# A fused two-block transformer kernel: where the modulation passes stand, a merge in two passes, earlier recurrence gates, and other seams

## The chip, the core and the metric

The kernel runs on one NeuronCore of a Trainium2 chip. A core has five engines with instruction streams of their own: TensorE (PE, matrix products), VectorE (DVE), ScalarE (ACT), GpSimd (POOL) and SyncE (SP, which only issues transfers here). They meet through semaphores. The metric is the device time of one execution in microseconds (us), lower is better.

## What is computed

One sequence of 512 positions with 1024 channels passes through two blocks. Everything is float32.

```python
h  = modulate(rms(x, norm1_g), sh1, sc1); p = h @ w_in      # mod = silu(c) @ w_mod + b_mod
q, k, v = mla_qkv(p, ...)                                   # 8 heads, keys of the context beside them
x = x + g1 * ((sig(p_ga) * (attend(q, k, v) @ w_o) + sig(p_gb) * (fft2(p_f) @ w_fourier)) @ w_out)
h2 = modulate(rms(x, norm2_g), sh2, sc2)
x = x + g2 * expert_choice(h2, w_router, w_e_gate, w_e_up, w_e_down)   # 16 experts, 64 tokens each
z = rms(x, norm1_g_2) @ w_in_2                              # second block
u = causal_dwconv(z_x, 4) + b;  r, i = sig(u @ wa + ba), sig(u @ wx + bx)
y = [rg_lru(u, r, i) * gelu(z_gate), z_b * causal_dwconv(z_c * z_sx, 3)]
x = x + y @ w_out_2
x = x + (gelu(dwconv(gate)) * dwconv(up)) @ w_down_2;  out = rms(x, final_g_2)
```

## The kernel before

Each float32 factor of a large product is split into a high part, which ACT casts, and the rest, which DVE subtracts (`split`, and `Stream.ahead` for weights that come tile by tile: `w.h` is the `wih`, `w2h` of the trace, `w.l` is `wil`, `w2l`). `mm3` (L138) then makes three matmuls of each product, low times high, high times high, high times low (L141 to L143). A tile of 128 output channels by 512 positions is 24 matmuls of 512 columns, and needs both parts of its weights. The order on every engine is the order in which the code is written, and each engine executes its own stream strictly in that order.

`mix_in` (from 110 to 256 us) makes the tiles of `w_in`: `fcol(0..3)`, then `gate(8..15)`, each through `mtile` (L523), with the steps of q, k and v between them (`nat`, `s2`, `s3`, `s4`) and, between the gates, the two steps of the Fourier part (`ustep`, `ystep`). Beside that DVE makes 32 modulation passes: `mod_rest` (L455) fetches the vector c over ACT's queue as `sc`, ACT takes its sigmoid (`sce`), and each call of `parts` multiplies one row block `wm` of `w_mod` with `sc` and sums it into `mo` (L481). Three buffers of `wm` are in flight; SP fetches the next when a pass has freed one. `finish` adds the bias, turns `mo` on PE (L496) and stores rows that `merge` reads later.

`attention` follows, with `fourier(m)` (the Fourier output product) in its first part; `merge` (372 to 438 us) multiplies by `w_o` and `w_out`; then router, top-16 selection, gather, and 16 experts in pairs, whose weights stream in as tiles over SP's queue: 41 of them are issued at fixed points before the indices are known (`EW`, `ew_issue`), the others after. `scatter_last` closes the experts and prepares the second block's input.

`mix2` starts with eight tiles of the recurrence (`lru_in`, L1514): product, bias and convolution of four taps (ACT, then three DVE steps), split of the result, and three tiles later `gates` (six matmuls, two sigmoids, one product). There are two PSUM banks for `gates` and six for tiles. `short` makes the short convolutions, `lru1`, `lru2` the scan, `gated(0..7)` the last eight tiles. `ffn` makes 48 tiles and then the down product with eight accumulating banks.

All SBUF tiles are placed by hand: `PLAN` holds one address for each allocation, and a tile that takes memory of an older one waits for the older one's last reader.

## Time and profile before

| | us |
|---|---|
| median of 3 runs (1351.0 to 1352.37) | 1351.12 |
| the profiled execution | 1354.08 |
| its span | 1352.3 |
| PE busy | 1276.3 (94% of the span) |
| DVE busy | 720.6 (53%) |
| ACT busy | 509.0 (38%) |

The profiled execution is 3.0 us longer than the median, and 1.8 us of it lie outside the span. PE is the engine that is nearly always busy, so the 76 us in which it is not, and the stretches in which its clock is granted at half (PEclk 0.50, which is 1.2 GHz instead of 2.4), are what can be had back without removing work. A row of the waits names the instruction that waited, the instruction that released it, and the time. An engine other than PE matters where PE waits for it.

### The profile page before, as it was taken

The numbers are of one execution on the slowest core, as the hardware profiler recorded it, in microseconds if no ns is written. First come the engines' busy times: TensorE is split into PE (matmuls) and PEld (weight loads), VectorE is DVE, ScalarE is ACT, GpSimd is POOL, SyncE is SP. The second block draws the span as 40 slices with busy tenths as digits, with TensorE's granted clock in tenths as the row PEclk, the third lists the DMA queues.
The fourth block names the chain that finished last, engine by engine and source line by source line (L and its number), as shares of the span: only waits on it lengthen the run. The fifth ranks groups of instructions, "written<-read, shape, count | busy, mean of one in ns | idle before, by whom it ended". The sixth has DMA issues, their size and how long they took to land.

```text
span 1352.3 us, 16175 instructions
## 1 busy us (share of the span) xinstructions
PE 1276.3 (94%) x6418; PEld 962.8 (71%) x6418; DVE 720.6 (53%) x1099; ACT 509.0 (38%) x873; POOL 95.8 (7%) x141
## 2 busy tenths in 40 slices
PE   6999989999999399999888999999999999999997
PEld 4798867777687233433348888788988888878886
DVE  5646687678783612322257745843555555555323
ACT  5634442367633311111034466432333333344302
POOL 1223300000330000000010000000000000000002
PEclk9999989899999699999989999999999999999999
DMA  9510368220464999999950213330423202403201
GB/s 388 199 41 32 125 221 331 91 94 8 155 249 168 335 350 415 421 421 421 421 240 1 81 44 130 120 140 0 187 94 156 94 8 118 155 16 125 104 22 63
DMA packets 42844, 229.32 MB, mean 170 GB/s; under 512 B 5120, under 2 KB 5904, under 8 KB 23184
## 3 DMA queue, kind: packets, MB, share of 16 engines
q1 hardware_dynamic: 38736, 217.99, 41.4%
q10 hardware_dynamic: 2816, 6.08, 1.2%
q0 software_dynamic: 1216, 4.20, 0.9%
q8 instruction: 51, 0.84, 0.3%
q14 instruction: 25, 0.20, 0.0%
HBM read 224.05 MB, written 4.21 MB: 169 GB/s over the span
## 4 chain that ended last, share of the span: by engine, by line
PE 68%; DMA 8%; DVE 6%; ACT 3%; issue 1%; SPq 0%; POOLq 0%; POOL 0%; ACTq 0%; DVEq 0%
PE o L141 6%; PE o L143 6%; PE o L142 6%; PE mm L143 4%; PE mm L141 4%; PE mm L142 4%; DMA w_eu<-in_w_eu_dram 4%; PE d L1298 3%; PE u L142 3%; PE u L143 3%; PE u L141 3%; PE g L143 3%; PE g L142 3%; PE g L141 3%; DMA w_ed<-in_w_ed_dram 3%; PE g L1265 3%
## 5 line engine op out<-in xcount | busy, mean ns | idle before, releaser
L143 PE MATMUL mm<-hTh,w2l 128*128 128x512 f32 (+1 forms) x256 | 93.8, 367 | 2.5 <-DVE w2l L243 2.5
L141 PE MATMUL mm<-hTl,w2h 128*128 128x512 f32 (+1 forms) x256 | 94.2, 368 | 0.9 <-DVE hTl L150 0.8
L142 PE MATMUL mm<-hTh,w2h 128*128 128x512 f32 (+1 forms) x256 | 93.6, 365 | 0.0
L143 PE MATMUL g<-hTh,wul 128*128 128x512 f32 (+1 forms) x208 | 77.6, 373 | 0.5 <-DVE wul L243 0.5
L141 PE MATMUL g<-hTl,wuh 128*128 128x512 f32 (+1 forms) x208 | 77.6, 373 | 0.0
L143 PE MATMUL u<-hTh,wul 128*128 128x512 f32 (+1 forms) x208 | 77.6, 373 | 0.0
L141 PE MATMUL u<-hTl,wuh 128*128 128x512 f32 (+1 forms) x208 | 77.6, 373 | 0.0
L142 PE MATMUL g<-hTh,wuh 128*128 128x512 f32 (+1 forms) x208 | 77.5, 373 | 0.0
L142 PE MATMUL u<-hTh,wuh 128*128 128x512 f32 (+1 forms) x208 | 77.5, 373 | 0.0
L141 PE MATMUL o<-wdl,gsh 128*128 128x512 f32 x192 | 74.8, 389 | 1.1 <-DVE cv L1724 1.1
L142 PE MATMUL o<-wdh,gsh 128*128 128x512 f32 x192 | 74.7, 389 | 0.0
L143 PE MATMUL o<-wdh,gsl 128*128 128x512 f32 x192 | 74.7, 389 | 0.0
L1724 DVE SCALAR_TENSOR_TENSOR cv<-u,pvt,cv 128x510 f32<-128x510 f32 (+1 forms) x48 | 36.0, 749 | 65.5 <-ACT cv L1721 64.6
L1265 PE MATMUL u<-w_eu,xeT 128*64 128x512 f32 x256 | 58.9, 594 | 5.7 <-DMA w_eu<-in_w_eu_dram 5.7
L1265 PE MATMUL g<-w_eg,xeT 128*64 128x512 f32 x256 | 59.7, 603 | 2.7 <-DMA w_eg<-in_w_eg_dram 2.6
L1298 PE MATMUL d<-w_ed,ehT 128*64 128x512 f32 x256 | 59.4, 610 | 2.7 <-ACT ehT L1284 2.4
L1724 DVE SCALAR_TENSOR_TENSOR cv<-g,pvt,cv 128x510 f32<-128x510 f32 (+1 forms) x48 | 35.9, 749 | 45.4 <-ACT cv L1721 44.5
L243 DVE TENSOR_TENSOR wul<-wur,wuh 128x1024 fp32r<-128x1024 f32 x48 | 58.3, 1217 | 2.2 <-ACT wuh L242 1.8
L1275 DVE TENSOR_TENSOR h<-h,u 128x512 f32<-128x512 f32 x8 | 5.5, 688 | 96.7 <-PE u L1265 96.7
L143 PEld LDWEIGHTS mm<-hTh,w2l 128*128 128x128 f32 x256 | 49.1, 192 | 11.1 <-DVE w2l L243 3.5
L143 PE MATMUL mm<-hTh,wil 128*128 128x512 f32 x128 | 52.1, 407 | 5.0 <-DVE wil L243 5.0
L141 PE MATMUL mm<-hTl,wih 128*128 128x512 f32 x128 | 52.3, 409 | 4.0 <-ACT wih L242 4.0
(437 smaller groups left out, 3047.2 us busy)
## 6 DMA issues: line engine op xcount, KB each, us to landing
w_eg<-in_w_eg_dram SPq DMA_DIRECT2D x24, 1024.0 KB, 15.6
w_eu<-in_w_eu_dram SPq DMA_DIRECT2D x24, 1024.0 KB, 17.0
w_ed<-in_w_ed_dram SPq DMA_DIRECT2D x24, 1024.0 KB, 19.8
wur<-in_w_up_dram SPq DMA_DIRECT2D x24, 1024.0 KB, 6.0
wm<-in_w_modT_dram SPq DMA_DIRECT2D x32, 512.0 KB, 5.2
w2r<-in_w_in_dram SPq DMA_DIRECT2D x14, 1024.0 KB, 5.9
wdr<-in_w_down_dram SPq DMA_DIRECT2D x12, 1024.0 KB, 4.8
wir<-in_w_inT_dram SPq DMA_DIRECT2D x10, 1024.0 KB, 7.2
```

Of the source, the lines that this page charges most:

```text
L141: mm(ps, ah, bl, start=first, stop=False)
L142: mm(ps, ah, bh, start=False, stop=False)
L143: mm(ps, al, bh, start=False, stop=last)
L243: (lo or K.nc.vector).tensor_sub(w.l, src, w.h.bitcast(F32))
L1265: nc.tensor.matmul(p[64 * e:64 * e + 64, :], xT[:, k, 64 * e:64 * e + 64], w[e + k // m * 2][:, 512 * (k % m):512 * (k % m) + 512], start= ...
L1275: nc.vector.tensor_tensor(h, h, ps["w_eu"], op=OP.mult)
L1298: nc.tensor.matmul(p[64 * e:64 * e + 64, 512 * n:512 * n + 512], hT[:, k, 64 * e:64 * e + 64], w[k // m * 2 + e][:, 1024 * (k % m) + 512 * ...
L1724: nc.vector.scalar_tensor_tensor(v[:, s:T], ps[:, 0:T - s], f[:, k:k + 1], v[:, s:T], op0=OP.mult, op1=OP.add)
```

## The change

No arithmetic is taken out. What moves:

- `mod_rest` (the fetch of `sc`, its sigmoid and product) is called after `nat(3)` instead of at the third step of the `fcol` loop; the first three `wm` loads stay at that step (`mod_first`). The 32 passes stand between a tile's weight split and its eviction: none, none, one, three in `fcol(0..3)`, one in `gate(8)`, three in each of `gate(9..15)`, and the last six in `fourier(0..5)`. The bias follows `fourier(5)`, the turn of `mo` (`mod_finish`) the fifth attention item.
- The raw weights of `w_in` are loaded a tile earlier; `cpos` is loaded at step 3 and split after `gate(8)`; the tile pool of this part has four banks instead of three.
- `merge` makes the first half of `w_out`'s columns in two passes over the four banks; the splits and the routing steps are spread anew, and `EW` changes its portions (41 in both).
- `idle` issues five and later three matmuls that nothing reads, after the router rows and after the index matmuls.
- `scatter_last` splits the second tile of `w_in_2` ahead of `rows(2)` and `rows(3)`. In `lru_in`, `gates(j - 3)` stands right behind the tile's product, ahead of its convolution. One more tile of `w_in_2` is split ahead of the square roots. In the last stage the eight banks are used in another order.
- `PLAN` is new throughout.

On ACT, after `nat(3)` (`kT` copies the turned keys out of the bank `tr`, `v` is the value copy), before:

```order
L578 ACTIVATE sq_1085,s_124_1086<-a_1035 128x32
L697 ACTIVATE kT_1099<-tr_1103,pvt 96x2x128
L697 ACTIVATE kT_1100<-tr_1103,pvt 96x2x128
L697 ACTIVATE kT_1101<-tr_1103,pvt 96x2x128
L697 ACTIVATE kT_1102<-tr_1103,pvt 96x2x128
L610 COPY v_643<-a_1121 128x512
L614 ACTIVATE sq_1136<-a_1121 128x512
```

and now:

```order
L586 ACTIVATE sq_1087,s_125_1088<-a_1037 128x32
L462 DMA sc_1105<-in_crow_dram 128x1024
L463 ACTIVATE sce_1106<-sc_1105 128x1024
L705 ACTIVATE kT_1110<-tr_1114,pvt 96x2x128
L705 ACTIVATE kT_1111<-tr_1114,pvt 96x2x128
L705 ACTIVATE kT_1112<-tr_1114,pvt 96x2x128
L705 ACTIVATE kT_1113<-tr_1114,pvt 96x2x128
L618 COPY v_643<-a_1132 128x512
L622 ACTIVATE sq_1147<-a_1132 128x512
```

The fetch and the sigmoid that waits for it stand ahead of the four copies out of `tr`; before, they stood 42 rows later.

On DVE, at `gate(8)` (`wm` is a modulation pass, `cpl` the split of `cpos`, `wil` the split of a `w_in` tile, `ul` the Fourier part), before:

```order
L481 SCALAR_TENSOR_TENSOR wm_1569,mo_1559<-wm_1569,sc_1560 128x1024
L481 SCALAR_TENSOR_TENSOR wm_1657,mo_1559<-wm_1657,sc_1560 128x1024
L481 SCALAR_TENSOR_TENSOR wm_1660,mo_1559<-wm_1660,sc_1560 128x1024
L174 TENSOR_TENSOR cpl_1740<-cpr_1737,cph_1739 128x1024
L174 TENSOR_TENSOR cpl_1746<-cpr_1743,cph_1745 128x1024
L243 TENSOR_TENSOR wil_1757<-wir_1662,wih_1756 128x1024
L481 SCALAR_TENSOR_TENSOR wm_1729,mo_1559<-wm_1729,sc_1560 128x1024
L481 SCALAR_TENSOR_TENSOR wm_1732,mo_1559<-wm_1732,sc_1560 128x1024
L150 TENSOR_TENSOR ul_1795<-u_1793,uh_1794 128x1024
```

and now:

```order
L243 TENSOR_TENSOR wil_1745<-wir_1581,wih_1744 128x1024
L481 SCALAR_TENSOR_TENSOR wm_1670,mo_1104<-wm_1670,sc_1105 128x1024
L174 TENSOR_TENSOR cpl_1781<-cpr_1661,cph_1780 128x1024
L174 TENSOR_TENSOR cpl_1785<-cpr_1663,cph_1784 128x1024
L150 TENSOR_TENSOR ul_1790<-u_1788,uh_1789 128x1024
L243 TENSOR_TENSOR wil_1806<-wir_1748,wih_1805 128x1024
L481 SCALAR_TENSOR_TENSOR wm_1673,mo_1104<-wm_1673,sc_1105 128x1024
L481 SCALAR_TENSOR_TENSOR wm_1676,mo_1104<-wm_1676,sc_1105 128x1024
L481 SCALAR_TENSOR_TENSOR wm_1751,mo_1104<-wm_1751,sc_1105 128x1024
L153 SCALAR_TENSOR_TENSOR y4l_1337<-mm_1844,y4h_1336 128x2x256
```

One pass, not three, and the two `cpl` splits now precede the `ul` and the split of the next tile; the next three passes stand behind that split.

On ACT, in the recurrence's input loop (`gt` are the gate sigmoids, `xi` the tile's eviction, `xihlh` its cast, `w2h` the cast for the tile after next), before:

```order
L1517 ACTIVATE xi_5671<-mm_5397,pvt 128x512
L1520 CAST xihlh_5676<-xi_5671 128x512
L1523 CAST lwh_5392<-lwr_5390 128x256
L1535 ACT_TABLE_LOAD
L1535 ACTIVATE gt_5686<-gt_5682,pvt 128x512
L1535 ACTIVATE gt_5692<-gt_5688,pvt 128x512
L242 CAST w2h_5698<-w2r_5532 128x1024
L1517 ACTIVATE xi_5726<-mm_5695,pvt 128x512
```

and now:

```order
L1574 ACT_TABLE_LOAD
L1574 ACTIVATE gt_5684<-gt_5680,pvt 128x512
L1574 ACTIVATE gt_5690<-gt_5686,pvt 128x512
L1556 ACTIVATE xi_5693<-mm_5406,pvt 128x512
L1559 CAST xihlh_5698<-xi_5693 128x512
L1562 CAST lwh_5401<-lwr_5399 128x256
L242 CAST w2h_5707<-w2r_5541 128x1024
L1574 ACTIVATE gt_5739<-gt_5735,pvt 128x512
L1574 ACTIVATE gt_5745<-gt_5741,pvt 128x512
```

The table load and the two sigmoids moved ahead of the eviction of the fourth tile (`xi_5671`, now `xi_5693`), and the cast `w2h` moved behind that tile's casts.

The diff, cut to its core (of `PLAN` one line of each side):

```diff
 ARENA = 204 * 1024
-EW = (13, 4, 4, 6, 12, 0, 2)
+EW = (16, 4, 5, 3, 11, 0, 2)
...
-        def finish(P, tag):
+        def bias():
...
             nc.vector.scalar_tensor_tensor(mo[:, 2], mo[:, 2], 1.0, self.pv("n2g"), op0=OP.add, op1=OP.mult)
+        def finish(P, tag):
...
-        for _ in range(3):
-            load()
+        def first():
+            for _ in range(3):
+                load()
         self.sh2c, self.a2c = mo[:, 1], mo[:, 2]
-        return parts, finish
+        self.mod_parts, self.mod_bias, self.mod_finish, self.mod_first = parts, bias, finish, first
...
-        def mtile(i, P):
+        def mtile(i, P, parts=0):
             w = wst.get(i)
+            if i % 2 == 0:
+                wst.load(i // 2 + 1)
+            if parts:
+                self.mod_parts(parts)
...
-        def gate(i, P):
-            self.sigmoid(i, mtile(i + 4 * (i // 8), P))
+        def gate(i, P, parts=0):
+            self.sigmoid(i, mtile(i + 4 * (i // 8), P, parts))
...
-            ps = mtile(8 + g, P)
+            ps = mtile(8 + g, P, (0, 0, 1, 3)[g])
...
             A.free(w)
+        self.mod_rest()
...
                 f(t)
-            if i > 2:
-                parts(i - 1)
+            if i == 3:
+                cpr = [self.load(I["cpos"][b], [128, 2, 512], "cp") for b in range(2)]
...
                 A.free(wq, wkv)
-                parts, finish = self.mod_rest()
+                self.mod_first()
...
         A.free(tabs, rg, gq)
-        cp = [self.split(I["cpos"][i], [128, 2, 512], "cp") for i in range(2)]
...
         st = ExitStack()
-        P = Psum(self.tc, st, "pF", {"mm": (1, 3), "u": (2, 2), "m": (1, 1)})
+        P = Psum(self.tc, st, "pF", {"mm": (1, 4), "u": (2, 2)})
...
         for i in range(8):
-            gate(8 + i, P)
-            parts(2)
+            gate(8 + i, P, 3 if i else 1)
+            if i == 0:
+                cp = [self.split(None, [128, 2, 512], "cp", raw=r) for r in cpr]
+            if i == 6:
+                wfs = self.Stream(self, [I["w_fourier"][i] for i in range(2)], 4, "wfo", look=2)
+                wfs.load(0)
+                wfs.load(1)
+            if i == 7:
+                wfs.ahead(1)
             (ystep if i % 2 else ustep)(i // 2)
-            parts(2)
...
                 A.free(self.hTb, *cp)
-                wfs = self.Stream(self, [I["w_fourier"][i] for i in range(2)], 4, "wfo", look=2)
-                wfs.ahead(1)
-        finish(P, "m")
...
                 w = self.wfs.get(m)
+                if m < 6:
+                    self.mod_parts(1)
...
                 fourier(m)
+                if m == 5:
+                    self.mod_bias()
...
                     soft(items[i + 2])
+                if i == 4:
+                    self.mod_finish(P, "pt")
...
                     mgsplit(m - 1)
-                if m >= 4:
+                if m in (5, 7):
...
-            def out(t, n, lo, hi, steps):
-                ps = P("o")[:, 0:hi - lo]
+            def out(t, n, lo, hi, steps, ks=range(NK)):
+                if ks[0] == 0:
+                    acc[t] = P("o")
+                ps = acc[t][:, 0:hi - lo]
                 c, d = slice(128 * (t % 2), 128 * (t % 2) + 128), slice(lo, hi)
-                for k in range(NK):
+                for k in ks:
...
                     self.mm3(ps, m.h[:, c], m.l[:, c], w.h[:, k % 2, d], w.l[:, k % 2, d], k == 0, k == NK - 1)
+                if ks[-1] < NK - 1:
+                    return
...
+            acc = {}
+            for t in range(NT):
+                out(t, 0, 0, 512, {2: [(wsplit, t // 2)]}, range(NK // 2))
+            A.free(*wout[0][0:2])
...
                     steps = {k: [] for k in range(NK)}
-                    if (n, t) != (0, 0):
-                        u, b = (t - 1, n) if t else (NT - 1, 0)
-                        steps[4].append((route, u, 4 * b, 4))
-                        steps[7].append((route1, u, 4 * b))
+                    for k, f, u, b in {(0, 2): [(5, route, 0, 0)], (0, 3): [(4, route1, 0, 0), (5, route, 1, 0)],
+                                       (1, 0): [(0, route1, 1, 0), (1, route, 2, 0), (4, route1, 2, 0), (5, route, 3, 0)],
+                                       (1, 1): [(0, route1, 3, 0), (4, route, 0, 4), (7, route1, 0, 4)],
+                                       (1, 2): [(4, route, 1, 4), (7, route1, 1, 4)],
+                                       (1, 3): [(4, route, 2, 4), (7, route1, 2, 4)]}.get((n, t), []):
+                        steps[k].append((f, u, b, 4) if f is route else (f, u, b))
                     if n == 0:
-                        steps[1].append((wsplit, 1))
-                        out(t, 0, 0, 512, steps)
-                        if t == 1:
+                        if t % 2 == 0:
+                            steps[5].append((wsplit, 1))
+                        out(t, 0, 0, 512, steps, range(NK // 2, NK))
+                        if t == 0:
...
                         if t == NT - 1:
-                            for w in wout[0]:
-                                A.free(w)
+                            A.free(*wout[0][2:4])
...
             self.probe("x1", x)
+            warm = next(iter(self.ew.values()))
+            def idle(n):
+                ps = P("mm")
+                for _ in range(n):
+                    nc.tensor.matmul(ps, self.ident, warm[:, 0:512], start=True, stop=True)
+            idle(5)
...
                 nc.vector.tensor_copy(la[q], pa[q, 0:2 * NE].rearrange("p (b j i) -> p i b j", b=2, i=2)[:, i])
+            idle(3)
...
                 self.n_turn(P, "tr", 1, self.hTg)
+                self.ws2.ahead(1)
...
                 rows(3)
-                self.ws2.ahead(1)
...
                 ps = mtile(j)
+                if j > 2:
+                    gates(j - 3)
...
                 lru_in(j)
-                if j > 2:
-                    gates(j - 3)
...
                 lru1(2 * j + 1)
-            ws.ahead(22)
+            ws.ahead(23)
+            ws.look = 2
...
             P = Psum(self.tc, st, "pJ", {"o": (1, 8)})
-            acc = [[P("o") for n in range(2)] for t in range(NT)]
+            acc = [P("o") for i in range(2 * NT)]
+            acc = acc[:2] + acc[3:] + acc[2:3]
+            acc = [acc[2 * t:2 * t + 2] for t in range(NT)]
...
 PLAN = [
-    1, 299, 308, 25, 175, 242, 341, 316, 358, 33, 9, 220, 267, 283, 59, 139, 143, 0, 58, 333, 99, 266, 49, 376, 144, 1,
...
+    0, 352, 137, 129, 216, 8, 161, 145, 360, 260, 286, 328, 53, 200, 70, 258, 284, 179, 285, 9, 95, 8, 178, 216, 376,
...
```

## Rows read from the trace of the kernel before

**Rows 1.** PE's waits, whole run: engine, line, releaser: us in total, times, longest.
```profile
PE mm L143 <- DVE wil L243: 5.0, 5, 3.2
PE mm L141 <- ACT wih L242: 4.0, 3, 2.4
PE gt L141 <- ACT gt L1535: 2.9, 1, 2.9
PE m L496 <- DVE mo L491: 2.7, 1, 2.7
PE mm L143 <- DVE w2l L243: 2.5, 2, 1.7
```
**Rows 2.** Timeline of PE: start, us, instruction [idle before, releaser]; three waits of mix_in.
```profile
172.11 0.61 PE L141 MATMUL mm<-hTl,wih 128*128 128x512 f32 x1 [2.41 <-ACT wih L242]
...
194.35 0.50 PE L143 MATMUL mm<-hTh,wil 128*128 128x512 f32 x1 [3.23 <-DVE wil L243]
194.68 0.39 PE L141 MATMUL mm<-hTl,wih 128*128 128x512 f32 x1
194.91 0.39 PE L142 MATMUL mm<-hTh,wih 128*128 128x512 f32 x1
...
235.66 0.50 PE L141 MATMUL mm<-hTl,wih 128*128 128x512 f32 x1 [1.19 <-ACT wih L242]
```
**Rows 3.** Timeline of ACT around the modulation vector.
```profile
169.76 1.06 ACT L463 ACTIVATE sce<-sc 128x1024 f32<-128x1024 f32 x1 [5.74 <-DMA sc<-in_crow_dram]
```
**Rows 4.** Stretches: bounds, us, busy PE, PEld, DVE, ACT, POOL, PEclk, DMA share, GB/s.
```profile
172.40:179.20 6.80, 6.29 (x15) 4.41 (x15) 5.96 (x19) 3.01 (x6) 0.00 (x0) 0.50 0.80 298
257.70:261.10 3.40, 3.40 (x10) 2.62 (x9) 1.10 (x3) 3.40 (x7) 1.37 (x2) 0.50 0.02 2
372.00:438.00 66.00, 65.73 (x345) 51.74 (x343) 38.68 (x55) 22.58 (x46) 12.70 (x15) 1.00 0.57 205
448.84:472.73 23.89, 5.16 (x23) 3.03 (x25) 15.67 (x72) 6.62 (x15) 1.32 (x2) 0.50 0.97 347
474.00:484.00 10.00, 10.00 (x50) 3.23 (x46) 0.00 (x0) 0.61 (x2) 1.78 (x2) 1.00 0.81 284
742.40:745.80 3.40, 3.31 (x8) 2.63 (x9) 2.51 (x3) 2.23 (x4) 0.00 (x0) 0.50 0.00 0
```
**Rows 5.** Timelines of ACT, then PE, at the point to which mod_rest goes.
```profile
118.33 1.54 ACT L697 ACTIVATE kT<-tr,pvt 96x256 f32<-96x256 f32 x4
...
122.47 0.71 PE L594 MATMUL tr<-ident,craw 128*128 128x128 f32 x5
```
**Rows 6.** DMA issued in 1205 to 1222: queue, count, KB each, us to landing.
```profile
fg<-in_fg_dram ACTq DMA_DIRECT2D x1, 512.0 KB, 3.5
```
**Rows 7.** Groups of DVE in 168 to 256.43: count, busy us, mean ns, idle before.
```profile
L481 DVE SCALAR_TENSOR_TENSOR wm<-wm,sc 128x1024 f32<-128x1024 f32 x32 | 37.8, 1215 | 0.0
```
**Rows 8.** Timelines of ACT, DVE and PE in the input loop of the recurrence.
```profile
740.46 1.28 ACT L1535 ACT_TABLE_LOAD   x1
741.75 1.26 ACT L1535 ACTIVATE gt<-gt,pvt 128x512 f32<-128x512 f32 x2
...
743.98 1.23 DVE L243 TENSOR_TENSOR w2l<-w2r,w2h 128x1024 fp32r<-128x1024 f32 x1 [0.24 <-ACT w2h L242]
...
745.22 0.63 PE L141 MATMUL mm<-hTl,w2h 128*128 128x512 f32 x1
```
**Rows 9.** Timeline of DVE at the start of the second block.
```profile
713.33 1.22 DVE L243 TENSOR_TENSOR w2l<-w2r,w2h 128x1024 fp32r<-128x1024 f32 x1
```
**Rows 10.** Timelines of PE and DVE at the recurrence's output.
```profile
853.97 0.50 PE L143 MATMUL mm<-hTh,w2l 128*128 128x512 f32 x1 [1.75 <-DVE w2l L243]
...
857.67 1.20 DVE L243 TENSOR_TENSOR w2l<-w2r,w2h 128x1024 fp32r<-128x1024 f32 x1
```
**Rows 11.** Timeline of PE at the last stage's start.
```profile
1215.79 0.47 PE L141 MATMUL o<-wdl,gsh 128*128 128x512 f32 x1 [1.08 <-DVE cv L1724]
```
**Rows 12.** Timeline of PE at the experts' first work.
```profile
468.74 1.97 PE L1244 MATMUL tr<-ident,xe 128*128 128x128 f32 x8 [6.08 <-DMA xe<-h2d,idx]
```

86 rows, old and new, of the table PLAN are left out of this document.

## The prediction

> **What bounds the kernel now.** I first read the grouped waits of PE [rows 1], since the kernel spends 1276.3 of its 1352.3 us with PE busy, and then followed each long wait into the timelines of the engine that released it. Five groups belong to the places that the change touches: the weight splits of `mix_in` (5.0 and 4.0 us), the turn of `mo` (2.7), the recurrence gates (2.9) and the splits of the second block's input tiles (2.5, of which 1.75 is one wait [rows 10]). A sixth is the 1.08 us at the start of the last stage [rows 11]. Then I looked at the granted clock: after the longer waits there are stretches at 0.50 [rows 4], in which a busy PE does half its work. The 6.80 us behind the 2.41-us wait at 172.11 cost 3.1 us, since PE was busy for 6.29 of them; the 3.40 us behind the turn of `mo`, and a like stretch at 237.21 behind a wait for a split, cost 1.7 each. Everything below is counted on PE's path; DVE and ACT count where PE waits for them.
>
> **Modulation passes in `mix_in`.** The work is the same 32 passes of 1.2 us [rows 7], so only their places matter. The wait at 172.11 [rows 2] goes back to ACT, which had stood 5.74 us for the fetch of `sc`, until 169.76 [rows 3], with PE's next weights to be cast behind that. With the fetch made earlier, this wait goes, and its clock loss. The 3.23 us at 194.35 [rows 2] come from three passes and two `cpl` splits that stood ahead of a needed `wil`; the two splits, 2.4 us, now follow that `wil`, and what the three passes leave of the wait is in the cost below. The third wait, 1.2 us at 235.66, with its half clock, came from four passes a gate, and there are three now. The turn of `mo` leaves PE's path, since attention hides it: 2.74 us and its half clock. Removed: 2.4 + 3.2 + 1.2 + 2.7 = 9.5 us of waits, and 3.1 + 1.7 + 1.7 = 6.5 us of clock, 16.0 in all. The other 2.1 us of the three groups [rows 1] are waits of 0.2 to 0.5 us between steps that depend on each other; I leave them.
>
> What it costs: ACT now issues the fetch right after the last square of `nat(3)`, at about 118.4, and waits. Queued behind it are the four copies that empty the bank `tr` (1.54 us from 118.33 [rows 5]), and PE's transposes of `s2(2)`, at 122.47 in the same bank, wait for these. A fetch of the same size over the same queue, on quiet DMA, landed in 3.5 us [rows 6]; beside other loads ACT stood 5.7 for it [rows 3]. With the first, the sigmoid (1.06 us) ends at 123.1, the copies at 124.6, and PE waits 2.2 us; with the second, 4.4. I take 2.2, as few loads run there. Waits of 2.4 and 2.7 us were followed by half clock, so I add 1.7. Second, DVE still has one pass, two `cpl` splits and `ul` ahead of the `wil` of `gate(9)`, some 4.8 us, and three passes ahead of the one before; the nearest row is the 3.23-us wait with five such steps in front, the other end is nothing; I take 1.5, somewhat under half. Later gates carry five steps of 1.2 us each (three passes, one `wil`, one `ul`), against two 24-matmul groups and more of PE's in the time of two gates: DVE ends ahead. The six passes in attention lie beside softmax work with three banks to run ahead, so nothing. Sum: 16.0 - 2.2 - 1.7 - 1.5 = **10.6 us less** (bounds 6 and 14).
>
> **Merge and router.** The stretch 372 to 438 has PE busy for 65.73 of 66.00 us [rows 4]. The same products in another order can't gain there, and the moved splits have the DVE and ACT time (38.68 and 22.58 of 66) to hide in: nothing, bounds 0 and +1. If that cover failed, it would cost one split, 1.2 us, at each pass. The `idle` matmuls lie inside the waits for the selection (the whole stretch 448.84 to 472.73 has PE busy for 5.16 us only) and for the gather (6.08 us [rows 12]); eight 128-column transposes take 1.97 us at half clock [rows 12], so 512 columns take some 1.0, and five and three of them fit. They could give back the clock for the first 4.0 us of experts, 2.0 us. But after the last of the three PE would still stand idle for about 3 us before the gather lands, and waits of 2.4 us and more had half clock behind them. I take nothing, bounds 0 and -2.0.
>
> Here the Trainium skill ("TensorE: Matmul & The Clock Gate", Part 1) speaks for the idle matmuls: the throttled state is the default, and activity releases it. By that rule the sum would be 2.0 us lower.
>
> **Experts.** The stream has holes after the indices: in 474 to 484 the DMA share is 0.81 [rows 4], which is 1.9 us of stream lost, and it thins before and after. With the new addresses the first loads after the indices wait for earlier experts' readers. PE later waits for that stream, so what is filled comes back. I take most of the 1.9, **1.5 us less**; bounds 0 and -3.8, twice the 1.9.
>
> **`scatter_last`.** Of the 2.5 us for `w2l` [rows 1], 2.5 - 1.75 = 0.76 are here. The second tile's split moves ahead of the rows, which shift by its 1.2 us, and with them their squares, on ACT and POOL, the scaled rows, and the split at 713.33 [rows 9] that stands behind them. That third split, done at 714.55, was wanted at once. PE arrives 0.76 us sooner and waits 0.7 there: **0.1 less**, bounds -0.8 and +0.5.
>
> **Gates ahead of the convolution.** The 2.9-us wait [rows 1] was for the first two sigmoids, and those now come early enough. But look at what is late next. PE's following tile needs `w2h`, cast on ACT, and `w2l` from DVE, done at 743.98 + 1.23 = 745.21, and PE began that tile at 745.22 [rows 8]. On ACT the same steps stand ahead of `w2h` in both orders: table load 1.28, two sigmoids 1.26, eviction, convolution, casts; they are only permuted. So `w2l` is again done at about 745.2. PE makes its gates 2.9 us sooner, starts the tile's first two products when `w2h` is there, and then stands. It is ahead by two matmuls, 0.5 us, and the half clock [rows 4], which before fell on the gates while `w2l` was late anyway, now falls on the tile, 1.1 us for the 2.2 us left of it. I take **0**, bounds -1.7 and +1.2. Had the wait simply gone, it would be 2.9 + 1.7 = 4.6.
>
> In this chain the sigmoid starts 0.01 us behind the end of the table load [rows 8]. The Trainium skill ("ScalarE: Activation LUTs", "What ACT_TABLE_LOAD costs") counts a drain of 1.38 us to a table switch beside the load's 1.28. The row shows no such drain ahead of the sigmoid. By the page an estimate of the sum would be 1.4 later, 1339.6; I give that 0.03, inside the forecast.
>
> **One more tile ahead of the square roots.** It removes the 1.75 us [rows 10], and pushes the square roots and everything behind them on ACT by one cast, about the 1.06 us of ACT's step of that size [rows 3]. The next tile's `w2l` still ends at 857.67 + 1.20 = 858.9, behind the same chain, and PE, 1.75 us earlier, wants it after 24 matmuls of 0.23 each (the starts at 194.68 and 194.91 [rows 2]): 853.97 - 1.75 + 5.6 = 857.8. It waits 1.1: **0.7 less**, bounds -1.8 and 0.
>
> **Last stage.** The 1.08 us [rows 11] were the third bank's, which waits for the last tile's convolution. The code puts the third allocated bank last, but banks are handed out as they come into use: in the program as built the third accumulation still writes the bank of that last tile and carries the same wait. **0**, bounds 0 and -1.1.
>
> **The sum**: -10.6 - 1.5 - 0.1 - 0 - 0.7 - 0 = -12.9 us. On the profiled execution: 1354.08 - 12.9 = 1341.2. That execution stands 3.0 above the median, so on the median 1351.1 - 12.9 = **1338.2**.
>
> **Rivals.** (a) Every removed wait is a full gain: 4.6 at the gates, 1.75 for the split ahead, 0.76 in `scatter_last`, 1.1 in the last stage, 8.2 together where I count 0.8, and the early fetch costs no clock (1.7): 1338.2 - 7.4 - 1.7 = 1329.1. For it: each edit has its wait in the rows. Against: the chains above. Chance 0.17. (b) The cover in the gates runs out: three passes ahead of an eviction hold a bank or `ul`, 0.8 us in each of eight gates, 6.4 in all: 1344.6. For it: DVE was the releaser of 5.0 us there already. Against: four passes a gate before, three now, and one bank more. Chance 0.20. (c) The idle matmuls bring back the clock: 2.0 less, 1336.2; chance 0.15, inside the forecast's range. (d) Slower: the new addresses. SP issues in order, and a `wm` load that waits for its buffer holds the `w_in` tile queued behind it. Four such tiles lie in the gates. If each lands late as `wil` was at 194.35, 3.2 us and 1.7 of clock, that is 4 x 4.9 = 19.7: 1357.9. It decides from 12.9 / 4 = 3.2 us for each tile. For it: all addresses are new. Against: the tiles are asked for one earlier, and DMA carries a pass less a gate. Chance 0.06. (e) The gains of `mix_in` are met by a wait that I don't see in attention, and little is left: 1349 to 1353, chance 0.06.
>
> **How the numbers follow.** My forecast, with (c) in it, holds 1333 to 1342 with 0.51. The range takes in (a) and (b): 1329 to 1345, leaving out (d), (e) and the edges of the others. A measurement of this kernel tells 0.2%, 2.7 us, from no change. Faster: 0.17 + 0.51 + 0.20 = 0.88; within: 0.06; slower: 0.06.
>
> **What would show it.** Right: no PE wait over 1 us between 160 and 256 but one at `gate(9)`; a new wait of about 2 us at `s2(2)`, released by the `kT` copies; the 2.9-us wait gone from `gt` and a like one on the next tile's `w2h` and `w2l`; the 1.08 us still at the last stage. Wrong: waits of every gate on `wil`, SP held on `wm`, or a tile in the recurrence that starts at once.

## The result and the profile after

The changed kernel takes 1332.93 us (median of four runs, 1329.48 to 1335.48) against 1351.7 for the kernel before (1351.0 to 1352.37) beside it: the ratio is 0.985, 95% interval 0.983 to 0.986. The forecast was 1338.2 with a range of 1329 to 1345, so the time is inside, and 5.3 us below the point. The profiled execution took 1333.91 with a span of 1331.8, that is 20.5 less than the span before, where the sum said 12.9; by the medians the gain is 18.8. The runs of the changed kernel lie 6 us apart, and the longest of them had a lower granted clock (0.985) than the shortest (0.990); so below the stretches of the profiles are compared, and medians only beside them.

The first view is again PE's waits over the whole run (engine, line, releaser: us in total, times, longest). These are the lines that answer to [rows 1], with two that were not of interest before:

```profile
PE mm L143 <- DVE w2l L243: 4.1, 3, 2.4
...
PE d L1335 <- ACT ehT L1321: 2.4, 1, 2.4
...
PE tr L602 <- ACT kT L705: 1.5, 1, 1.5
PE o L141 <- DVE cv L1762: 1.1, 1, 1.1
...
PE mm L143 <- DVE wil L243: 0.5, 1, 0.5
```

The waits for `wih` (4.0), `gt` (2.9) and `mo` (2.7) are gone, those for `wil` fell from 5.0 to 0.5. New is the one for `kT`, and those for `w2l` went up from 2.5 to 4.1. The wait for the gather fell from 6.1 [rows 12] to 0.7, since idle matmuls now stand in it. The second view is the timeline of PE at the waits that the prediction spoke of (start, us, instruction [idle before, releaser]):

```profile
126.26 0.77 PE L602 MATMUL tr<-ident,craw 128*128 128x128 f32 x5 [1.51 <-ACT kT L705]
...
188.62 0.50 PE L143 MATMUL mm<-hTh,wil 128*128 128x512 f32 x1 [0.49 <-DVE wil L243]
...
697.32 0.58 PE L143 MATMUL mm<-hTh,w2l 128*128 128x256 f32 x1 [2.37 <-DVE w2l L243]
...
838.47 0.50 PE L143 MATMUL mm<-hTh,w2l 128*128 128x512 f32 x1 [1.31 <-DVE w2l L243]
855.55 0.50 PE L143 MATMUL mm<-hTh,w2l 128*128 128x512 f32 x1 [0.45 <-DVE w2l L243]
...
1195.24 0.47 PE L141 MATMUL o<-wdl,gsh 128*128 128x512 f32 x1 [1.08 <-DVE cv L1762]
```

And DVE around the second of these waits, with PE's row at which the tile after that begins (`wil` is split one tile ahead, so the split at 187.34 is that of `gate(9)`, and the one at 193.03 that of `gate(10)`):

```profile
187.34 1.23 DVE L243 TENSOR_TENSOR wil<-wir,wih 128x1024 fp32r<-128x1024 f32 x1
...
189.62 2.35 DVE L174 TENSOR_TENSOR cpl<-cpr,cph 128x1024 fp32r<-128x1024 f32 x2
...
193.03 1.22 DVE L243 TENSOR_TENSOR wil<-wir,wih 128x1024 fp32r<-128x1024 f32 x1
...
196.65 0.40 PE L141 MATMUL mm<-hTl,wih 128*128 128x512 f32 x1
```

The third view is the table of stretches (bounds, us, busy PE, PEld, DVE, ACT, POOL, PEclk, DMA share, GB/s). The first row is the kernel before over `mix_in`, the other block is the changed kernel:

```profile
110.00:256.00 146.00, 134.58 (x705) 113.67 (x703) 106.25 (x197) 55.47 (x96) 21.71 (x19) 0.96 0.51 185
```
```profile
110.00:256.00 146.00, 144.00 (x780) 124.23 (x778) 114.21 (x208) 63.50 (x108) 22.93 (x20) 1.00 0.51 178
...
18.00:28.20 10.20, 9.57 (x40) 6.15 (x44) 4.97 (x11) 3.64 (x6) 0.00 (x0) 0.50 1.02 421
663.10:666.50 3.40, 2.89 (x8) 1.00 (x10) 1.62 (x2) 1.51 (x2) 0.00 (x0) 0.52 1.00 416
697.30:700.70 3.40, 3.38 (x16) 3.38 (x17) 2.29 (x3) 0.00 (x0) 0.00 (x0) 0.51 0.12 17
```

In the same 146 us PE is busy for 144.00 instead of 134.58, all of it at full clock. The half clock has left `mix_in`; among other places it is still there at the start (10.2 us here, 3.4 in the execution of before), behind the wait for `ehT`, and behind the new 2.37-us wait.

Cut at instructions that both kernels have, the span divides as follows. The marks are the ACT square on `a` at 108.41 (110.54 after), attention's first matmul, the Fourier output product `pt`, at 256.43 (242.37), the turn of `xe` [rows 12], PE's last wait for `ehT`, the first gate matmul of the recurrence, and the accumulation that waits in the last stage [rows 11].

| stretch | before | after | difference | the sum had |
|---|---|---|---|---|
| start | 108.41 | 110.54 | +2.1 | 0 |
| `mix_in` | 148.02 | 131.83 | -16.2 | -10.6 |
| attention, merge, router, gather | 212.31 | 212.56 | +0.3 | 0 |
| experts, to the wait for `ehT` | 212.22 | 208.68 | -3.5 | -1.5 |
| to the first gates (`scatter_last`) | 51.65 | 53.22 | +1.6 | -0.1 |
| first gates to the last stage | 483.18 | 478.41 | -4.8 | -0.7 |
| the rest | 136.51 | 136.56 | 0 | 0 |

So four terms are off in this execution: `mix_in` by 5.6, the experts by 2.0, the gates by 4.7, `scatter_last` by 1.7 the other way. Two of the rows scatter with the clock where the code is the same: over the profiles of the changed kernel and its variants the first mark lies between 108.4 and 113.6, and in the nine with this code `scatter_last` takes 50.3 to 53.2 us. The +2.1 and the +1.6 are therefore not shown to come from an edit.

### The profile page after: what moved, and what is told of

Read it like the earlier page. It is cut to its first block, busy times and chain, and to the rows that moved or that the text cites. A ratio compares the mean times of both kernels' runs of the same rounds, so it can differ in the third digit from the quotient of the medians.

```text
span 1331.8 us, 16233 instructions
## 1 busy us (share of the span) xinstructions
PE 1277.3 (96%) x6434; PEld 962.7 (72%) x6434; DVE 720.6 (54%) x1099; ACT 509.3 (38%) x873; POOL 99.1 (7%) x141
## 4 chain that ended last, share of the span: by engine, by line
PE 53%; DMA 7%; DVE 2%; ACT 2%; issue 1%; POOL 0%; POOLq 0%; SPq 0%; DVEq 0%; ACTq 0%
PE o L141 5%; PE o L143 5%; PE o L142 5%; PE g L143 3%; PE u L141 3%; PE u L143 3%; PE u L142 3%; PE g L141 3%; PE g L142 3%; DMA w_ed<-in_w_ed_dram 3%; PE mm L143 3%; PE mm L142 3%; PE mm L141 3%; PE g L1302 3%; PE d L1335 2%; PE u L1302 2%
## 5 line engine op out<-in xcount | busy, mean ns | idle before, releaser
L143 PEld LDWEIGHTS mm<-hTh,w2l 128*128 128x128 f32 x256 | 49.1, 192 | 12.5 <-DVE w2l L243 5.2
L141 PEld LDWEIGHTS mm<-hTl,w2h 128*128 128x128 f32 x256 | 49.0, 192 | 8.5 <-DVE hTl L150 1.0
L142 PEld LDWEIGHTS mm<-hTh,w2h 128*128 128x128 f32 x256 | 49.0, 191 | 7.6
```

What stands on the lines that cost most here:

```text
L141: mm(ps, ah, bl, start=first, stop=False)
L142: mm(ps, ah, bh, start=False, stop=False)
L143: mm(ps, al, bh, start=False, stop=last)
```

## The experiments

Each kernel below is the changed one with one edit, and with the few entries of `PLAN` fitted anew that the edit made collide. Ratios are to the kernel before on the same chip, with 95% intervals. The changed kernel was run again, on the chip on which its variants with the gates, `mod_rest` and `scatter_last` put back ran.

> The changed kernel itself, on the chip of these runs, as the measure for the others: 1329 to 1336 us. If the scatter of its runs comes from the clock (theory), its profiled execution differs from the first in stretches at half clock near the start (18 to 28 us) or in the experts, and in no wait by more than 0.3 us; the rival is that single waits of TensorE differ between executions.

Measured: 1332.4 us, ratio 0.985 (0.982 to 0.988), and a span of 1328.0 in the profile, 3.8 less than the first. At the start the half clock lasts 3.4 us instead of 10.2, and attention starts at 240.95 instead of 242.37. Behind the `ehT` wait there is none. Two waits do differ: the one at the third tile is 1.35 instead of 2.37, and the one for the turned rows 1.80 instead of 0.96, both next to a stretch whose clock differs. So each theory has a part: the clock differs, and so do waits beside it. From the `ehT` wait to the first gates this execution takes 50.7 us, the first one 53.2; the stretch from first gates to last stage is the same to 0.1 us in both.

**The gates.** Edit:

```diff
                 ps = mtile(j)
-                if j > 2:
-                    gates(j - 3)
...
                 lru_in(j)
+                if j > 2:
+                    gates(j - 3)
```

> The changed kernel with one part undone: `gates(j - 3)` stands behind the convolution again. Theory from the two traces (the `w2l` that the prediction thought late belongs to a tile after the next, so the whole wait was a gain): TensorE waits 2.9 us again for the first `gt`, a stretch at half clock follows, and the kernel takes 4.6 us more than the changed one's 1332.9, some 1337.5; between the first gates and `short` it is 4 to 5 us longer. Rival, the prediction's step (the wait only moves to the next tile's `w2l`): the same time, and the stretch from the gates to `short` within 1 us of the changed kernel's.

Measured: 1336.95 us, ratio 0.9865 (0.984 to 0.989). Timeline of PE in this kernel, and the stretch behind the wait (columns as above):

```profile
725.88 0.79 PE L141 MATMUL gt<-xihll,lwh 128*128 128x512 f32 x1 [2.99 <-ACT gt L1572]
```
```profile
725.90:729.30 3.40, 3.40 (x8) 2.72 (x9) 2.58 (x4) 2.12 (x3) 0.00 (x0) 0.51 0.00 0
```

The wait is back with its half clock, and from the first gates to the last stage the kernel takes 480.65 us (to the first `o` matmul; 480.58 in the kernel before) against 475.81 and 475.87 in the two executions of the changed one: 4.8 more. The rival, which was my step, is out. What happens there in the changed kernel (timelines of PE, ACT and DVE):

```profile
723.66 0.39 PE L141 MATMUL gt<-xihll,lwh 128*128 128x512 f32 x1
...
725.02 0.39 PE L141 MATMUL mm<-hTl,w2h 128*128 128x512 f32 x1
...
720.73 1.28 ACT L1574 ACT_TABLE_LOAD   x1
722.02 1.27 ACT L1574 ACTIVATE gt<-gt,pvt 128x512 f32<-128x512 f32 x2
...
728.31 1.22 DVE L243 TENSOR_TENSOR w2l<-w2r,w2h 128x1024 fp32r<-128x1024 f32 x1 [0.23 <-ACT w2h L242]
```

The gates and the next tile both start at once. The `w2l` that ends at 729.5 is made long after that tile has begun: it belongs to a tile further on, as the section on the change says of `w2h` ("for the tile after next").

**`mod_rest`.** Edit: the call goes from behind `nat(3)` back to the third step of the `fcol` loop, ahead of `mod_first`.

> The changed kernel with one part undone: `mod_rest` (the fetch of `sc` and its sigmoid) stands at the third step of the `fcol` loop again, just ahead of the first `wm` loads. Theory (ScalarE stands for the fetch and TensorE's next weights are cast behind it): a TensorE wait of 2 us or more for a `wih` or `wil` around 160 to 175 us with half clock behind (2.4 + 3.1 in the kernel before), while the 1.51 us wait for `kT` at 126 goes; 4 us longer than the changed kernel, some 1337. Rival (the fourth bank and the earlier loads of `w_in` already covered that stall, and the early fetch only costs its 1.5 us): 1 to 2 us shorter, 1331 to 1332.

Measured: 1338.4 us, ratio 0.988 (0.9855 to 0.990); attention starts at 246.93, 4.6 later than in the changed kernel with the same start, and 4.1 and 4.3 later than in two variants with that start. Timelines of PE and ACT in this kernel:

```profile
174.27 0.50 PE L141 MATMUL mm<-hTl,wih 128*128 128x512 f32 x1 [2.38 <-ACT wih L242]
175.76 0.79 PE L143 MATMUL mm<-hTh,wil 128*128 128x512 f32 x1 [0.76 <-DVE wil L243]
...
171.92 1.06 ACT L463 ACTIVATE sce<-sc 128x1024 f32<-128x1024 f32 x1 [5.70 <-DMA sc<-in_crow_dram]
```

The wait of [rows 2] is back at the same size although there is a fourth bank and an earlier load. The early fetch is worth 4.1 to 4.6 us net of its own cost, and the rival is out.

**The cost of the early fetch.** Edit:

```diff
         nc.scalar.dma_start(sc, I["crow"].to_broadcast([128, D]))
-        nc.scalar.activation(e, sc, AF.Sigmoid)
-        nc.vector.tensor_tensor(sc, sc, e, op=OP.mult)
...
         s2(2)
+        self.mod_silu()     # the two lines taken out above
```

> The changed kernel with the fetch of `sc` where it is now, but its sigmoid and product only after `s2(2)`. Theory (ScalarE's stand for the fetch is all that holds the four `kT` copies, and TensorE with them): the 1.51 us wait at 126 goes, some 1331.5, nothing appears later. Rival (another wait takes its place, since the next products need other copies from ScalarE): the same time, and a wait of 1 us or more within 10 us behind it.

Measured: 1331.5 us, ratio 0.984 (0.982 to 0.986). In the kernel before these copies started at 118.33 [rows 5]. Timelines of ACT in the changed kernel, then in this one:

```profile
123.71 1.06 ACT L463 ACTIVATE sce<-sc 128x1024 f32<-128x1024 f32 x1 [3.15 <-DMA sc<-in_crow_dram]
124.67 1.53 ACT L705 ACTIVATE kT<-tr,pvt 96x256 f32<-96x256 f32 x4
```
```profile
120.69 1.56 ACT L709 ACTIVATE kT<-tr,pvt 96x256 f32<-96x256 f32 x4
```

PE's wait at 126 is gone, nothing over 0.5 us stands in its place up to attention, which starts at 240.67, 1.7 earlier than in the changed kernel with the same 10.2 us of half clock at the start (2.0 and 2.2 earlier than in two variants with that start). So the early fetch cost its wait and at most 0.7 more. The medians are too coarse for this: kernels with the early sigmoid have 1331.9, 1332.4 and 1332.9.

**The idle matmuls.** Edit: `idle(5)` and `idle(3)` taken out.

> The changed kernel without the eight idle matmuls. Theory (they give back the clock for the first work of the experts): the first transposes and products of the experts run at half clock again for some 4 us, 2 us longer than the changed kernel, some 1335; the gather and the selection take as long as now. Rival, the prediction's step (idle matmuls change nothing, since TensorE stands again before the gather lands): the same time within 0.5 us.

Measured: 1334.6 us, ratio 0.986 (0.984 to 0.988), and 212.07 us from the turn of `xe` to the `ehT` wait, against 208.7 and 208.8 in the two executions of the changed kernel, 212.2 before, and 208.7 to 210.3 in the other variants. Timeline of PE and the stretch behind the turn in the changed kernel, then both in this one, then the stretch in the kernel before:

```profile
448.80 5.49 PE L1179 MATMUL mm<-w_eg,ident 128*128 128x512 f32 x6
454.93 1.10 PE L1281 MATMUL tr<-ident,xe 128*128 128x128 f32 x8 [0.65 <-DMA xe<-h2d,idx]
```
```profile
454.93:470.00 15.07, 14.95 (x72) 5.37 (x72) 1.58 (x4) 3.60 (x6) 2.84 (x3) 1.00 0.96 338
```
```profile
453.46 1.97 PE L1279 MATMUL tr<-ident,xe 128*128 128x128 f32 x8 [6.02 <-DMA xe<-h2d,idx]
```
```profile
453.46:469.00 15.54, 15.54 (x62) 5.89 (x64) 1.58 (x4) 3.60 (x6) 1.91 (x2) 0.81 0.83 263
```
```profile
468.74:484.00 15.26, 15.26 (x66) 5.99 (x68) 1.58 (x4) 3.60 (x6) 1.91 (x2) 0.87 0.86 303
```

Selection and gather take as long in both. Without the idle matmuls the first work is at half clock, as in [rows 12], and over 15 us behind the turn the DMA share is 0.83 instead of 0.96; before it was 0.86. The first 25 us behind the turn, in the kernel before, the changed one and this one:

```profile
468.74:493.74 25.00, 24.88 (x114) 9.56 (x116) 3.84 (x9) 5.32 (x10) 2.85 (x3) 0.92 0.88 318
```
```profile
454.93:479.93 25.00, 24.77 (x122) 9.20 (x124) 3.84 (x9) 5.92 (x11) 2.84 (x3) 1.00 0.98 372
```
```profile
453.46:478.46 25.00, 24.89 (x108) 9.37 (x110) 3.84 (x9) 5.32 (x10) 2.85 (x3) 0.88 0.89 314
```

From then on the share is 1.0 in all three (421 GB/s from 500 to 638 us in the changed kernel), and PE waits for the stream at the end, so what the stream loses at first stays lost. At 421 GB/s the 54 and 58 GB/s that are missing over these 25 us are 3.2 and 3.4 us of stream, an estimate from these rows; the stretch is 3.5 and 3.4 longer. The other variants take up to 1.7 us longer than the changed kernel here, of which the same reckoning gives at most 1.0; the rest stays open. That slower matmuls free the weight buffers later, and so hold the loads back, is the reading that fits; the buffers themselves were not tried. This kernel has the changed addresses and portions and still takes what the kernel before took, so these alone gave nothing.

The prediction had it that waits of 2.4 us and more are followed by half clock. Behind the 3.23 us of [rows 2] in the kernel before, the longest wait of `mix_in`, the clock was whole:

```profile
194.30:197.70 3.40, 3.35 (x15) 2.78 (x16) 3.40 (x6) 0.00 (x0) 0.00 (x0) 1.00 0.72 225
```

**The expert portions.** Edit: `EW = (13, 4, 4, 6, 12, 0, 2)` instead of `(16, 4, 5, 3, 11, 0, 2)`.

> The changed kernel with the old portions of the expert tiles issued ahead of the indices (13, 4, 4, 6, 12 instead of 16, 4, 5, 3, 11). Theory, the prediction's step (what counts are the addresses and the stream's holes after the indices, not the portions): within 0.5 us. Rival (the portions issued before carry the 3.5 us that the stretch from the gather to the end of the experts got shorter): 1.5 to 3.5 us longer, by new waits for `wd` or `wg` tiles.

Measured: 1331.9 us, ratio 0.984 (0.982 to 0.986); 208.74 us in the experts, the same as the changed kernel. The portions did nothing.

**`scatter_last`.** Edit: `self.ws2.ahead(1)` goes from ahead of `rows(2)` to behind `rows(3)`.

> The changed kernel with one part undone: in `scatter_last` the second tile's split follows `rows(3)` again. Theory from the two traces (the earlier split pushes the rows, and with them the third tile's split, which TensorE then waits 2.4 us for, with half clock behind): the wait at the third tile shrinks to under 1 us and that around 697 loses its half-clock stretch, while the second tile waits 0.7 again; from the turn of the hidden rows to the first `gates` 1 to 2 us shorter, in all 1331 to 1332. Rival, the prediction's step (a gain of 0.1 by the move): 0.1 us longer. Second rival: the 2.4 us are set by the scaled rows on GpSimd and the clock, not by the place of the split: no change at the third tile, and the second tile's wait is added, 0.7 us longer.

Measured: 1332.2 us, ratio 0.983 (0.981 to 0.986). From the `ehT` wait to the first gates 51.7 us, against 53.2 and 50.7 in the changed kernel, and against 52.4 in three other variants whose half clock lies as here but for one more stretch. Waits of PE in 655 to 705, of this kernel:

```profile
PE tr L1490 <- DVE hTl L150: 1.8, 1, 1.8
PE mm L141 <- ACT w2h L242: 1.6, 1, 1.6
...
PE mm L143 <- DVE w2l L243: 0.8, 1, 0.8
```

The third tile no longer waits, but the second one waits 1.6 + 0.8 = 2.4 us. With the split ahead of `rows(2)` the third tile waits 1.3 to 1.4 in eight of nine profiles, in which PE's first products there run at half clock, as in the kernel before; in the first profile of the changed kernel and in this one they run at full clock, and the wait is 2.4. So the wait has changed its tile, and its size goes with the clock ahead of it. The second rival had the wait on the second tile, but not that the third is then free. Whether the move costs anything is not settled: those nine profiles take 50.3 to 53.2 us there, 51.8 in the mean, against 51.7 here and 51.65 before.

**The third split.** Edit: `self.ws2.ahead(2)` added between `scale(2)` and `scale(3)`.

> The changed kernel with a step added in `scatter_last`: the third tile of `w_in_2` is split between `scale(2)` and `scale(3)`. Theory (the third tile's split stands on VectorE behind a scaled row that waits for GpSimd's square, and that alone makes TensorE's 2.4 us at 697): the wait falls to about 1.2 us or goes, its half-clock stretch too; 2 to 3.5 us shorter, some 1330. Rival (the row then comes 1.2 us later, and its turn and the product behind it wait for it instead): the same time, with a wait of about the same size on the turned rows.

Measured: 1331.0 us, ratio 0.983 (0.981 to 0.985). Timeline of DVE in the changed kernel, then in this one:

```profile
694.71 1.41 DVE L1479 SCALAR_TENSOR_TENSOR sq<-x,ss,n1g 128x512 f32<-128x512 f32 x2 [0.72 <-POOL ss L159]
696.05 1.22 DVE L243 TENSOR_TENSOR w2l<-w2r,w2h 128x1024 fp32r<-128x1024 f32 x1
```
```profile
696.69 1.21 DVE L243 TENSOR_TENSOR w2l<-w2r,w2h 128x1024 fp32r<-128x1024 f32 x1
698.35 1.42 DVE L1480 SCALAR_TENSOR_TENSOR sq<-x,ss,n1g 128x512 f32<-128x512 f32 x2 [0.44 <-POOL ss L159]
```

The split stands where DVE had waited for POOL, and PE's wait for it is gone, with nothing in its place. The stretch takes 50.80 us, against 52.36 in the variant with the gates put back and the same half clock: 1.6 less. The theory's 2 to 3.5 us were reckoned from the 2.37 of the first profile, where 1.3 to 1.4 is the usual wait.

**The square roots.** Edit: `ws.ahead(22)` instead of `ws.ahead(23)`.

> The changed kernel with one tile less of `w_in_2` split ahead of the square roots, as before. Theory from the two traces (the wait only moves to the next tile: 1.75 there before, 1.31 + 0.45 = 1.76 now): the waits of 1.31 and 0.45 become one of 1.75, and the kernel takes the same time within 0.3 us in the stretch from the first gates to the last stage. Rival, the prediction's step: 0.7 us longer. Second rival (the whole wait removed was a gain): 1.75 longer.

Measured: 1331.1 us, ratio 0.983 (0.981 to 0.985); from first gates to last stage 475.99 us against 475.81 and 475.87. In place of 1.31 and 0.45 there is one wait:

```profile
832.88 0.50 PE L143 MATMUL mm<-hTh,w2l 128*128 128x512 f32 x1 [1.97 <-DVE w2l L243]
```

The wait moves on by a tile and divides; the one more tile is worth 0.1 to 0.2 us. The theory is right, and both rivals are out.

**The banks of the last stage.** Edit:

```diff
-            acc = acc[:2] + acc[3:] + acc[2:3]
...
+                            if k == 0 and (t, n) == (1, 0):
+                                nc.vector.memset(acc[3][1][:, 0:1], 0.0)
```

> The changed kernel with the banks of the last stage in their natural order and one written element that makes the third accumulation take another bank than that of the last tile's convolution. Theory, the prediction's step (banks are handed out as they come into use, so the reordered list still gives the third accumulation the last tile's bank, and the 1.08 us stays for that reason): the wait of 1.08 us at 1195 goes and the stretch from the start of the last stage to the end is 1 us shorter, some 1332. Rival (the 1.08 us are the time in which the last tile's product is finished by VectorE, whatever bank follows): the wait stands, or moves to the next accumulation, and nothing is gained.

Measured: 1333.0 us, ratio 0.984 (0.983 to 0.986); the last stage takes 1.0 longer, not shorter. Timelines of PE and DVE:

```profile
1198.53 0.47 PE L141 MATMUL o<-wdl,gsh 128*128 128x512 f32 x1 [2.03 <-DVE o L1816]
...
1194.82 2.29 DVE L174 TENSOR_TENSOR wdl<-wdr,wdh 128x2048 fp32r<-128x2048 f32 x1
1197.03 1.29 DVE L1739 TENSOR_TENSOR gsl<-gt,gsh 128x512 fp32r<-128x512 f32 x2
...
1198.32 0.06 DVE L1816 MEMSET o<- 128x1 f32 x1
```

The third accumulation runs without a wait, so the 1.08 us were that bank's. But the written element, 0.06 us in itself, stands on DVE behind a weight split of 2.29 and two of `gsl`, and the fourth accumulation waits 2.03 for it. My edit put a worse wait in the place of the first; the gain of 1.1 is not shown. An element written ahead of these splits was not tried.

**The steps joined.** First the sigmoid behind `s2(2)`, the third split and the bank together, then with this ahead of the last down product as well:

```diff
+                if last:
+                    pi = P("g")
+                    for _ in range(2):
+                        nc.tensor.matmul(pi, self.ident, w[0][:, 0:512], start=True, stop=True)
                 p = P("d")
```

> The changed kernel with the three steps joined that had a gain or should have one: the sigmoid after `s2(2)`, the third tile's split between the scaled rows, the other bank in the last stage. Theory (the three lie on TensorE's path one after the other, so they add): 1.5 to 1.7 at `s2(2)`, 1.6 at the third tile, 1.1 in the last stage, 4.2 to 4.4 less than the changed kernel: 1328.3 on the median. Rival (what is gained ahead of the experts is met by their stream, which sets its own end): the first gain is lost by the wait for `ehT`, 2.7 less.

> The kernel of the three joined steps with two idle matmuls of 512 columns more, ahead of the last down product, inside the 2.39-us wait for `ehT`. Theory (a wait of that length lets the clock fall for the next 3.4 us in some executions, 1.7 us each time, and idle matmuls inside the wait prevent it): no half-clock stretch between 660 and 668 in the profile, and 0.9 to 1.7 less than without them on the median, 1327; the wait itself shrinks to 0.6. Rival (the stretch comes from elsewhere, or the idle matmuls end later than `ehT` is there): the same time, or up to 0.5 longer.

Measured: 1329.2 us, ratio 0.982 (0.980 to 0.983), and 1327.45 us, ratio 0.981 (0.979 to 0.982). The first is 3.2 to 3.7 below the changed kernel, not 4.2 to 4.4. The bank costs here too: from the last stage's first accumulation to the end its profile takes 141.66 us and that of the second kernel 140.09, against 139.1 in the changed one. The rest of the difference stays open, since the medians come from different chips and runs of one kernel differ by 6 us, so that the rival's 2.7 is not excluded either. In its stretch to the first gates it takes 50.85 us, as with the third split alone; the second takes 49.1. Timeline of PE and a stretch in the second:

```profile
658.44 1.88 PE L1340 MATMUL g<-w_ed,ident 128*128 128x512 f32 x4
660.99 7.09 PE L1344 MATMUL d<-w_ed,ehT 128*64 128x512 f32 x32 [0.67 <-ACT ehT L1326]
```
```profile
651.00:668.00 17.00, 16.33 (x72) 5.42 (x72) 3.99 (x5) 2.58 (x3) 0.00 (x0) 1.00 1.01 419
```

The wait is filled and the clock stays whole. Since three of twelve profiles without these two matmuls show a whole clock there too, one profile doesn't prove the cause; the medians are 1.7 apart, as the theory has it, but their intervals overlap. This kernel has the lowest median of the study.

## Why the prediction came out as it did

- **`mix_in`, what was removed.** Right. All four waits and the three stretches at half clock went, and with `mod_rest` put back the first came back at 2.38 + 0.76. The other three were not put back one by one; that they went with the steps that stood ahead of them is read from the traces.
- **`mix_in`, what it costs.** Right for the fetch, wrong for the backlog, and too high in size: 5.4 taken, 2.0 measured. The wait at `s2(2)` is released by the `kT` copies behind the fetch, as told, but is 1.51 instead of 2.2 (1.44 to 1.78 over nine profiles), and the 1.7 of clock didn't come. At `gate(9)` there is 0.49 instead of 1.5, and not by the steps that I named: the pass, the two `cpl` splits and `ul` stand behind the split of `gate(9)`, at 187.34, and ahead of that of `gate(10)`, which ends 2.4 us before its tile begins at 196.65. As at the gates below, I gave a split to the tile ahead of its own. These 3.4 us too much leave 2.2 of the 5.6, and they are the small waits that I had left in the sum: 2.1 us in [rows 1], of which none is left.
- **Merge.** Right within its bounds of 0 and +1: from attention to the gather it is 0.3 us longer. PE now waits 1.0 us there for `woutl`, a split of `w_out`; the list of before has no such wait. The two passes were not put back alone.
- **The idle matmuls.** Wrong. I took 0, rival (c) with 2.0 was right, and a little small: the experts took 1.8 to 3.4 us longer without them. The step that failed is the size of one idle matmul. I took 1.0 us from the transposes of [rows 12], so that three would end 3 us ahead of the gather. Three took 5.49, 1.83 each at half clock, and ended 0.65 ahead of it. The premise behind it, that a wait of 2.4 us or more has half clock behind it, does not hold either, as the full clock behind the 3.23 us of [rows 2] shows; what 3 us of standing would have done here was not tried. Over some 15 us behind the turn the granted clock is 1.00 with the idle matmuls and 0.81 without. Here the trace agrees with the Trainium skill ("TensorE: Matmul & The Clock Gate", Part 1), by whose rule that activity releases the throttle the sum would have been 2.0 lower.
- **Experts.** Wrong in its cause. The hole in the stream did close, from 318 to 372 GB/s over the 25 us behind the turn, which by the estimate above is 3.2 of the 3.5 us. But I gave 1.5 of it to the new addresses, and without the idle matmuls these leave 314 GB/s and 212.07 us, where the kernel before took 212.22: some 0.1. The hole goes with the clock, and this term and the one above are one.
- **`scatter_last`.** Right in its path, too small in the wait, and its worth not settled. I followed the rows and the third split, let PE arrive 0.76 sooner, and had it wait 0.7. In the profiled execution it wanted the third `w2l` 7.63 us behind the first product instead of 9.89, since 3.4 us at half clock (704.8 to 708.2 before) had gone as well, and the split was as late as ever: 2.37 of waiting, with half clock behind. Where the half clock stayed on these products, in eight other profiles, the wait is 1.3 to 1.4. The term was 1.7 off in the profiled execution, but in the mean of nine the stretch is 51.8 against 51.65 before, so neither my -0.1 nor the +1.6 of the table is shown.
- **Gates.** Wrong, by 4.7 us. The step that failed is whose split it was: I took the `w2l` that ends at 745.21 [rows 8] for that of the tile begun at 745.22, because the two times met. Splits run two tiles ahead here; the tile in question had its weights, as the one at 725.02 has in the changed kernel, 4.5 us before the `w2l` made there ends. The sentence "Had the wait simply gone, it would be 2.9 + 1.7 = 4.6" was the right one, to 0.2 us, and my own sign of being wrong, a tile in the recurrence that starts at once, is what the trace shows. The sigmoid again starts 0.01 us behind the end of the table load, without a drain.
- **Square roots.** Right that the wait passes to the next tile. I had it at 1.1, it is 1.31 and a second of 0.45 on the tile behind: nothing gained instead of 0.7.
- **Last stage.** Right: the wait stands at 1.08, and with another bank the third accumulation no longer waits.
- **Rivals.** (a), every wait a full gain at 1329.1, was right in its largest term, the gates, and in the clock that the early fetch did not cost, and wrong in the other three. (b), (d) and (e) showed in no row: no gate waits on `wil` beyond 0.49, no tile of `w_in` is late, and attention to the gather takes 0.3 us longer, not 10 or more.

The errors partly cancel: 5.6 + 2.0 + 4.7 too little gain, against 1.7 + 0.7 + 0.3 too much and 2.1 us at the start, where the half clock lasted 6.8 us longer and which no edit touches. That the time lies inside the range is in part luck: with the first three errors alone it would have been 1338.2 - 12.3 = 1325.9, below the 1329.

## What to carry to other kernels

Two times that meet in a trace are not yet a dependence: where weights are prepared several tiles ahead, find by name or by count which tile a split belongs to before costing a wait as moved rather than removed. Work that fills a wait can pay where a stream lies behind it: here the clock came back and with it the hole in the stream closed. Size such work by its own kind of instruction. And compare one execution with another only where the half clock lies alike, or over several profiles. A wait at a point where DVE, POOL and PE meet can change its tile when code is moved by one step, as it did here: put the needed step into the hole in which the other engine stands, as with the third split, and not merely earlier.

## What was not expected of the hardware

- An idle matmul of 512 float32 columns against the float32 identity shows as two records and takes 0.94 us at full clock (four records in 1.88) and 1.83 at half (six in 5.49), about what eight transposes, 1024 columns in all, take (1.10 at full clock, 1.97 at half).
- The half clock is not the same from one execution of a program to the next. At the start it lasted 3.4, 10.2, and once 17.1 us, and attention began 1.4 to 2.2 us later with 10.2 than with 3.4, the code up to there being the same. Behind the same 2.39-us wait for `ehT` nine of twelve profiles show a stretch of 3.4 us at half clock, and three show none. The wait for `kT`, 1.44 to 1.78 us in nine profiles, was followed by none in any profile, nor was the 3.23-us wait at 194.35 in the kernel before, while the one of 1.19 us at 235.66 [rows 2] was. So the length of the wait alone does not tell, in these profiles, whether the clock falls.
